# A chunked delta-rule scan: the recurrence's values transposed for four chunks at a time

## The chip, the cores and the metric

The kernel runs on one core of one Trainium2 chip, as one program. The metric is the device time of one execution in microseconds (us), the median over several. TensorE (PE in the profile) multiplies matrices into PSUM; VectorE (DVE), ScalarE (ACT) and GpSimd (POOL) do the elementwise work and the copies; transfers are issued from the queues of SyncE (SP), ACT and POOL.

## The reference

One encoder block on 512 frames of 1024 values, batch 1, float32. What matters here is the middle of it, where two token mixers run on one projection:

```
x = x + 1/2 * SwiGLU(RMSNorm(x))                    (first FFN)
p = RMSNorm(x) @ W_in
y_A = RWKV7(token-shifted columns of p) @ P_A       (8 heads x 64)
y_B = ForgettingAttention(other columns) @ P_B      (8 heads x 64)
x = x + (sigmoid(g_A)*y_A + sigmoid(g_B)*y_B) @ W_out
x = x + 1/2 * SwiGLU(RMSNorm(x))                    (second FFN)
out = RMSNorm(x)

RWKV7, per head, frame by frame, with a 64x64 state S:
S_t = S_{t-1} diag(w_t) + (S_{t-1} a_t) b_t^T + v_t k_t^T
y_t = S_t r_t
```

## The kernel before

**The stages.** In the order of time: the first FFN, the projection W_in with the preparation of the mixers' operands, the **scan** (the recurrence in chunks, with the attention and the last columns of the projection woven into it), the output projections, the second FFN. Float32 products are computed as three products of float32r parts: each weight tile is cast (`whi`, ACT, line 133) and its rest is formed (`wlo`, DVE, line 134), and `mm3` (line 142) multiplies high by high, high by low and low by high.

**The scan.** The 512 frames are cut into 16 chunks of 32 frames (`C` = 32, `NC` = 16), and heads into four pairs (`NP` = 4). For all heads at once the inverse of a triangular 32x32 matrix per chunk is formed ahead of it on DVE (lines 1249 to 1254, tile `TT`), written to memory and read back in another layout (line 1255 to `Td`, line 1261 into `Tall`). Then the loop over the chunks c does on PE: `read` (`xps`, line 1565: what the state and the values say at this chunk), `ups` (line 1611: times the inverse), `sps` (line 1638: the next state) and `yps` (line 1644: the output). The operand of `sps`, `yps` and `xps` is a tile `R` of 128 partitions per head, which holds the state, the solved rows and the values of the chunk. There are four such tiles, `Rs[0]` to `Rs[3]` (the names `RD` in the profile), used in turn, and four `Ds` for keys and decay.

**The values.** They lie transposed, features by frames, in the tiles `vs` (`V` in the profile). `stage_v(c)` transposes on PE the values of chunks c and c+1 for the four pairs of heads (four transposes of 64 frames into the PSUM tile `vp`, line 1366) and ACT copies them from there into two tiles `R` (four copies of 32 partitions by 256 elements, line 1370). `stage_b(c)` does the like for keys (`bp`, lines 1375 and 1379). `staged(c)` calls the one for even c and the other for odd c, two chunks ahead: `stage_v` runs at c = 0, 2, 4, ... 12 for the chunks 2, 4, 6, ... 14, and once before the loop for chunk 0. For c = 1, 2, 6 and 10 the call stands before `read(c)`, for c = 4 behind the first products of the iteration, otherwise ahead of them.

**What is woven in.** `some(n)` issues n steps of three matmuls of the remaining projections: 13 tasks of 8 steps, four `pq` and nine `pgt`, whose weights are cast and split one task ahead. The attention of one pair of heads runs in three units; a unit's logits (`lp`, line 1438) and softmax weights (`pts`, an exponential on ACT in line 1449, here called *the exponentials*) belong to one iteration, its transposes (`turned`, line 1463), copies (`tr`, line 1468) and values (line 1477) to the next. Small work that belongs to none of these (casts and splits of weights, evacuations, normalisation) waits in a list `side` and is issued by `flush`.

**What sets the order.** The matmuls of the scan are kept in program order; the instructions of the other engines are ordered by a scheduler from their dependences and its own estimates, at build time. Each engine then works through its own list in that fixed order. `tc.issue_after(i)` puts the instructions of its block that run on i's engine behind i. PSUM tiles of the scan come from a pool of three banks (`pr`): a new tile waits until the tile three allocations earlier has been read.

Of the kernel before, what the change touches and what calls it, by code (L numbers as in the profile page):

```python
# [9 lines left out]
F32 = mybir.dt.float32  # L10
F32R = mybir.dt.float32r
BF16 = mybir.dt.bfloat16
AF = mybir.ActivationFunctionType
# [5 lines left out]
P = 128  # L19
# [6 lines left out]
NP = DA // P  # L26
C = 32
NC = T // C
NB = T // P
# [22 lines left out]
def kernel(  # L52
# [7 lines left out]
    dve, act, pool, pe = nc.vector, nc.scalar, nc.gpsimd, nc.tensor  # L60
# [6 lines left out]
    pr = ctx.enter_context(tc.tile_pool(name="pr", bufs=3, space=PSUM))  # L67
# [11 lines left out]
    ident = cp.tile([P, P], F32, name="ident")  # L79
# [183 lines left out]
    with tc.tile_pool(name="x0", bufs=1) as x0:  # L263
        keep = tc.keep_in_program_order
# [436 lines left out]
    keep = tc.keep_in_program_order  # L701
# [310 lines left out]
    with ExitStack() as mx:  # L1012
        rp = mx.enter_context(tc.tile_pool(name="rp", bufs=1))
        sctx = ExitStack()
        sp = sctx.enter_context(tc.tile_pool(name="sp", bufs=1))
# [91 lines left out]
        vs = [V4[:, p] for p in range(NP)]  # L1107
# [141 lines left out]
        for t in range(C - 1):  # L1249
            n, m = t + 1, C - 1 - t  # L1250
# [7 lines left out]
        for i in range(2):  # L1258
            for q in range(2):
                o = i * 64 + q * C  # L1260
# [59 lines left out]
        for b in range(NB):  # L1320
            o = vts[b]
# [38 lines left out]

        keep = tc.keep_in_program_order

        def stage_v(c, keep=keep):
            vp = pr.tile([P, NP, 2, 64], F32, tag="b", name="vp")
            for p in range(NP):
                keep(pe.transpose(vp[0:64, p].rearrange("p a b -> p (a b)"), vs[p][:, c * C:(c + 2) * C], ident[:]))
            for j in range(2):
                for q in range(2):
                    o = 32 + (1 - q) * 64
                    act.copy(Rs[(c + j) % 4][o:o + 32, :, q, :], vp[j * C:(j + 1) * C, :, q, :])  # L1370

        def stage_b(c, keep=keep):
            bp = pr.tile([P, NP, 2, 64], F32, tag="b", name="bp")
# [48 lines left out]
        class Unit:  # L1422
# [19 lines left out]
            def weights(s):  # L1442
                for q in range(2):
                    pt, mx = pts[:, q], pairs[s.p][2][q]
                    for b in s.bl:
                        n, mb = (b + 1) * P, mx[:, b:b + 1]
                        l = s.lps[q][:, s.at[b]:s.at[b] + n]
                        dve.tensor_reduce(mb, l, axis=AX.X, op=ALU.max, negate=True)
                        act.activation(pt[:, s.at[b]:s.at[b] + n], l, AF.Exp, bias=mb, accum_out=mx[:, NB + b:NB + b + 1])

            def scaled(s):
                for q in range(2):
# [103 lines left out]
        for part in (stage_v, stage_b):  # L1556
            part(0, lambda i: i)
        some_of = [(2, 1, 3), (3, 3, 2)] + [(2, 1, 3), (3, 1, 2), (4, 2, 2), (2, 1, 3), (2, 1, 3), (2, 1, 3)] + [(4, 2, 2), (2, 1, 3), (2, 1, 3), (2, 1, 3), (4, 3, 3), (2, 1, 3), (2, 1, 3), (2, 1, 3)]

        def read(c):  # L1560
            R = Rs[c % 4]
            xps = pr.tile([P, 2, 64], F32, tag="b", name="xps")
            for p, q in heads():
                o = (p // 2) * 64 + q * C
                keep(pe.matmul(xps[o:o + C, p % 2, :], G[p][q][:, c, 0, :], R[:, p, q, :], start=True, stop=True,
                               tile_position=(0, o)))
            Xs = sp.tile([P, 2, 64], F32, tag="Xs", name="Xs", bufs=2)
            return Xs, dve.tensor_copy(Xs[:], xps[:])
# [12 lines left out]
        def unit(n):  # L1581
            return units[places.index(n)] if n in places else None

        def staged(c):
            if c + 2 < NC:
                (stage_b if c % 2 else stage_v)(c + 2 - c % 2)

        parted.extend((0, n, part) for n, part in enumerate(first_parts))
        with tc.issue_after(ahead.ins):
            Xs, taken = read(0)  # L1590
        for c in range(NC):
            R, Rn, Dt = Rs[c % 4], Rs[(c + 1) % 4], Ds[c % 4]
            cs = slice(c * C, (c + 1) * C)
            u, v = unit(c - 1), unit(c)
            n = some_of[c]
            late_logits = v and c == 12
            if c not in (1, 2, 4, 6, 10):
                staged(c)
            with tc.issue_after(taken.ins):
                flush(100 if c in (1, 12) else 5)  # L1600
            some(n[0])
            if c == 4:
                staged(c)
            if u:
                u.turned()
            elif c == 0:
# [49 lines left out]
            if c + 1 < NC:  # L1656
                Xs, taken = read(c + 1)
# [257 lines left out]
```

## Time and profile before

| | |
|---|---|
| time, median of 3 runs | 1135.68 us (1135.48 to 1136.68) |
| profiled execution, its own time | 1136.47 us |
| its span, first to last instruction | 1134.8 us |
| granted TensorE clock, mean | 0.998 |
| the scan's loop within the span | about 532 to 684 us |
| PE busy / DVE / ACT in 531 to 684 us (153 us) | 152.65 / 103.43 / 116.38 us |

How it is read: the span lies inside the time of the execution, 1.7 us shorter. PE's busy time is the time in which at least one matmul is in flight by a model of its ends; PEld is the loading of weights into the array, which precedes each matmul, and the idle times of PEld with what ended them show where PE's sequence stood. A row of the timeline gives start, duration, engine, line, operation, output and inputs, the count of merged instructions, and in brackets the idle time before it with its releaser.

### The profile page before, as it was taken

The page shows a single profiled execution, that of the slowest core. Times are in us where ns is not written, and L with a number is a line of the kernel's source. Part 1 is how long each engine was busy: PE and PEld are TensorE (multiplying, and loading weights), DVE is VectorE, ACT ScalarE, POOL GpSimd, SP SyncE. Part 2 cuts the span into 40 slices and gives each one's busy share as a digit, 9 for nine tenths or more (in the row PEclk, how much of TensorE's full clock was granted, in tenths as well). Part 3 has the DMA queues.
Part 4 walks back from the last instruction along what each step waited for, and adds up shares of the span by engine and source line. Part 5 has one row for each costly group of instructions (what it writes and reads, how often), then busy time and mean ns, then how long its engine had stood idle before and what let it go on. Part 6 is the DMA issues. An engine that isn't in the chain of part 4 may idle for free.

```text
span 1134.8 us, 19652 instructions
## 1 busy us (share of the span) xinstructions
PE 1125.1 (99%) x7782; PEld 990.5 (87%) x7782; DVE 865.3 (76%) x1372; ACT 614.1 (54%) x1029; POOL 98.6 (9%) x168
## 2 busy tenths in 40 slices
PE   9999999999999999999999999999999999999997
PEld 7899999988887888888777777888999999988887
DVE  6889999977666888767776668879999999943243
ACT  6646655643345754355877757536555566532121
POOL 2000000010000111321000011132000000010000
PEclk9999999999999999999999999999999999999999
DMA  8433333353333333345113136544333333363322
GB/s 261 135 93 96 111 112 96 111 176 121 118 111 112 101 105 101 113 140 144 33 44 104 64 113 202 176 148 127 97 100 105 111 96 112 107 193 92 90 78 75
DMA packets 211018, 131.17 MB, mean 116 GB/s; under 512 B 10446, under 2 KB 201486, under 8 KB 210926
## 3 DMA queue, kind: packets, MB, share of 16 engines
q1 hardware_dynamic: 202366, 108.67, 32.9%
q0 software_dynamic: 6320, 20.45, 5.4%
q8 instruction: 61, 1.00, 0.4%
q10 hardware_dynamic: 2240, 0.79, 0.3%
q14 instruction: 31, 0.25, 0.1%
HBM read 115.02 MB, written 14.88 MB: 114 GB/s over the span
## 4 chain that ended last, share of the span: by engine, by line
PE 96%; DVE 1%; ACT 1%; DMA 1%; issue 0%; SPq 0%; DVEq 0%; ACTq 0%
PE za L142 23%; PE pd L142 17%; PE zc L142 14%; PE pgt L142 8%; PE pk L142 6%; PE ppj L1691 4%; PE pw L142 4%; PE pq L142 3%; PE pb L142 3%; PE pa L142 3%; PE pv L142 2%; PE pl L142 1%; DMA xin<-in_x_dram 1%; PE lp L1477 1%; PE gp L1206 1%; PE lp L1463 1%
## 5 line engine op out<-in xcount | busy, mean ns | idle before, releaser
L133 ACT CAST whi<-raw 128x1024 fp32r<-128x1024 f32 (+2 forms) x114 | 110.6, 971 | 178.9 <-PE pd L142 88.1
L134 DVE TENSOR_TENSOR wlo<-raw,whi 128x1024 fp32r<-128x1024 f32 (+2 forms) x114 | 128.3, 1125 | 73.2 <-ACT whi L133 72.8
L142 PE MATMUL pd<-hh,wlo 128*128 128x512 f32 (+1 forms) x272 | 100.5, 370 | 0.0
L142 PE MATMUL pd<-hh,whi 128*128 128x512 f32 (+1 forms) x272 | 100.1, 368 | 0.0
L142 PE MATMUL pd<-hl,whi 128*128 128x512 f32 (+1 forms) x272 | 100.0, 368 | 0.0
L142 PE MATMUL zc<-xh,whi 128*128 128x256 f32 x296 | 83.8, 283 | 0.0
L142 PE MATMUL zc<-xl,whi 128*128 128x256 f32 x296 | 83.8, 283 | 0.0
L142 PE MATMUL zc<-xh,wlo 128*128 128x256 f32 x296 | 83.8, 283 | 0.0
L142 PEld LDWEIGHTS pd<-hl,whi 128*128 128x128 f32 x272 | 51.3, 189 | 8.4
L142 PEld LDWEIGHTS pd<-hh,wlo 128*128 128x128 f32 x272 | 51.3, 189 | 8.1
L142 PEld LDWEIGHTS pd<-hh,whi 128*128 128x128 f32 x272 | 51.3, 189 | 8.0
L504 ACT CAST wtwo<-wsum 128x1024 fp32r<-128x1024 f32 x37 | 38.9, 1050 | 33.3 <-PE za L142 33.3
L142 PEld LDWEIGHTS zc<-xh,whi 128*128 128x128 f32 x296 | 56.8, 192 | 0.0
L142 PEld LDWEIGHTS zc<-xl,whi 128*128 128x128 f32 x296 | 56.8, 192 | 0.0
L142 PEld LDWEIGHTS zc<-xh,wlo 128*128 128x128 f32 x296 | 56.8, 192 | 0.0
L142 PE MATMUL pgt<-xh,whi 128*128 128x512 f32 x128 | 53.0, 414 | 0.0
L507 DVE TENSOR_TENSOR wlo<-raw,whi 128x1024 fp32r<-128x1024 f32 x41 | 50.0, 1219 | 2.5 <-ACT whi L504 2.5
L516 DVE TENSOR_TENSOR wsum<-wsum,raw 128x512 f32<-128x512 f32 x74 | 50.9, 688 | 1.2
L516 DVE TENSOR_TENSOR wsum<-raw 128x512 f32<-128x512 f32 x74 | 50.6, 684 | 0.0
L142 PE MATMUL pgt<-xh,wlo 128*128 128x512 f32 x128 | 50.2, 392 | 0.0
L142 PE MATMUL pgt<-xl,whi 128*128 128x512 f32 x128 | 50.0, 391 | 0.0
L504 ACT CAST whi<-raw 128x1024 fp32r<-128x1024 f32 x41 | 43.1, 1052 | 9.0 <-PE zc L142 8.1
(582 smaller groups left out, 3490.8 us busy)
## 6 DMA issues: line engine op xcount, KB each, us to landing
raw<-in_ffn_w_dram SPq DMA_DIRECT2D x118, 512.0 KB
raw<-in_w_in_dram SPq DMA_DIRECT2D x40, 512.0 KB
raw<-in_ffn_w_dram SPq DMA_DIRECT2D x15, 384.0 KB
xP<-xpark POOLq DMA_DIRECT2D x16, 256.0 KB, 4.9
raw<-in_w_out_dram SPq DMA_DIRECT2D x8, 512.0 KB
gsave<-gs SPq DMA_DIRECT2D x9, 256.0 KB
xin<-in_x_dram SPq DMA_DIRECT2D x4, 512.0 KB
xpark<-xT POOLq DMA_DIRECT2D x8, 256.0 KB, 5.9
```

The costliest lines, as they stand in the source:

```text
L133: marks["wide"] = act.copy(hi[:], raw[:])
L134: marks["rest"] = (eng or dve).tensor_tensor(lo[:], raw[:], hi[:].bitcast(F32), op=ALU.subtract)
L142: mm = pe.matmul(ps, w, x_, start=first and n == 0, stop=last and n == 2, skip_group_check=chain)
L504: keep(act.copy(dst, src))
L507: keep(dve.tensor_tensor(dst, src, f32(hi), op=ALU.subtract))
L516: keep(dve.tensor_tensor(to, a, b, op=ALU.add))
L1206: gm = pe.matmul(gps[g][o, c], BK[s, cc], G[p][q][s, cc], start=True, stop=True)
L1463: keep(pe.transpose(s.lps[q][:, k * P:(k + 1) * P], pts[:, q, k * P:(k + 1) * P], ident[:]))
L1477: keep(pe.matmul(av[half(q), j * P:(j + 1) * P], vt[k][:, h * 64:(h + 1) * 64], s.trs[q][:, o:o + P], start=k == 0, stop=k == b))
L1691: keep(pe.matmul(ps[:], a[:, k, :], y[k][b], start=k == 0 and n == 0, stop=k == NP - 1 and n == 2))
```

## The change

`stage_v` transposes the values of four chunks at a time, for c divisible by four: the PSUM tile `vp` is now written on all 128 partitions. ACT copies the first two chunks from it as before, and DVE copies the other half (64 partitions by 512 elements) into a new SBUF tile `vkept`, from which ACT fills the `R` tiles of the other two chunks when `stage_v` is called for them. The call for c = 4, which now has no transposes, moves to the head of the iteration. Beside that, in iterations with an attention unit the block of `flush` stands behind the last exponential of the unit before, so that ACT work which `flush` issues comes later in ACT's order than that exponential.

```diff
+        vkept = []
         def stage_v(c, keep=keep):
-            vp = pr.tile([P, NP, 2, 64], F32, tag="b", name="vp")
-            for p in range(NP):
-                keep(pe.transpose(vp[0:64, p]..., vs[p][:, c * C:(c + 2) * C], ident[:]))
+            if c % 4 == 0:
+                vp = pr.tile([P, NP, 2, 64], F32, tag="b", name="vp")
+                for p in range(NP):
+                    keep(pe.transpose(vp[:, p]..., vs[p][:, c * C:(c + 4) * C], ident[:]))
+                src = vp
+            else:
+                src = vkept.pop()
             for j in range(2):
+                i = (c + j) % 4
                 for q in range(2):
                     o = 32 + (1 - q) * 64
-                    act.copy(Rs[(c + j) % 4][o:o + 32, :, q, :], vp[j * C:(j + 1) * C, :, q, :])
+                    act.copy(Rs[i][o:o + 32, :, q, :], src[i * C:(i + 1) * C, :, q, :])
+            if c % 4 == 0:
+                kept = sp.tile([P, NP, 2, 64], F32, name="vkept", tag="vkept")
+                dve.tensor_copy(kept[64:128], vp[64:128])
+                vkept.append(kept)
...
-                        act.activation(pt[...], l, AF.Exp, bias=mb, accum_out=...)
+                        s.exp = act.activation(pt[...], l, AF.Exp, bias=mb, accum_out=...)
...
-            if c not in (1, 2, 4, 6, 10):
+            if c not in (1, 2, 6, 10):
                 staged(c)
-            with tc.issue_after(taken.ins):
+            with tc.issue_after(taken.ins), tc.issue_after(u.exp.ins) if u else ExitStack():
                 flush(100 if c in (1, 12) else 5)
             some(n[0])
-            if c == 4:
-                staged(c)
```

The change was announced as joined to the first FFN's second product in pairs of output tiles; the diff holds nothing of that, and outside the preparation of the scan and the scan itself the instructions stand in the same order in both kernels.

What it does to the order of instructions, at three places. On PE the only difference in the whole program are the transposes `vp`: 32 before, 16 now, all other matmuls in the same order. At the head of iteration c = 0 (`xps` is the last of `read(0)`, `pq` the first woven product), before:

```order
L1565 MATMUL xps<-RD_5396,G_3854 32x64
L1565 MATMUL xps<-RD_5396,G_3855 32x64
L1366 MATMUL vp<-ident,V_4016 64x128 x4
L142 MATMUL pq<-xh_3768,whi 128x512
L142 MATMUL pq<-xl_3769,whi 128x512
```

and now:

```order
L1576 MATMUL xps<-RD_5396,G_3854 32x64
L1576 MATMUL xps<-RD_5396,G_3855 32x64
L142 MATMUL pq<-xh_3768,whi 128x512
L142 MATMUL pq<-xl_3769,whi 128x512
L142 MATMUL pq<-xh_3768,wlo 128x512
```

The four transposes are gone there; the same holds at c = 4, 8 and 12.

On DVE, at the end of the inversion ahead of the scan (`TT` is its result, `wlo` the rest of a weight of the projection), before:

```order
L1252 TENSOR_TENSOR prod<-TT,Ls 128x31
L1254 TENSOR_TENSOR TT<-TT,prod 128x31
L1283 TENSOR_TENSOR qk_5202<-qk_5202,rstd 128x512
L1283 TENSOR_TENSOR qk_5235<-qk_5235,rstd 128x512
L1336 SCALAR_TENSOR_TENSOR nf<-la,nf 8x512
L134 TENSOR_TENSOR wlo<-raw,whi 128x1024
```

and now:

```order
L1252 TENSOR_TENSOR prod<-TT,Ls 128x31
L134 TENSOR_TENSOR wlo<-raw,whi 128x1024
L1254 TENSOR_TENSOR TT<-TT,prod 128x31
L1283 TENSOR_TENSOR qk_5202<-qk_5202,rstd 128x512
L1283 TENSOR_TENSOR qk_5235<-qk_5235,rstd 128x512
L1336 SCALAR_TENSOR_TENSOR nf<-la,nf 8x512
```

The rest `wlo` of one weight has moved ahead of the last step of the inversion (the first copy into `vkept` stands earlier in the same chain).

On ACT, from iteration c = 7 into c = 8 (`tr` copies attention weights, lines 1615 and 1616 copy the solved rows into `R`, lines 1401 and 1402 cast attention operands, 1449 are the exponentials), before:

```order
L133 CAST whi<-raw 128x1024
L1468 COPY tr<-lp 128x384 x2
L1615 COPY RD_5397<-ups 32x2x64
...
L1402 CAST qb_5420<-qk_5619 64x512
L1449 ACTIVATE pts,mx_5945<-lp,mx_5945 128x512
L1449 ACTIVATE pts,mx_5946<-lp,mx_5946 128x512
L1295 ACTIVATE qrn<-pq_6364,epsr 128x512
L1296 ACTIVATE qrn<-qrn 128x512
L1648 COPY V_4016<-yps 128x4x32
L1501 ACT_TABLE_LOAD
L1501 ACTIVATE gs<-gs 128x512
L1370 COPY RD_5397<-vp 32x4x64 x4
```

and now:

```order
L1479 COPY tr<-lp 128x384 x2
L1624 COPY RD_5397<-ups 32x2x64
...
L1460 ACTIVATE pts,mx_5944<-lp,mx_5944 128x512
L1460 ACTIVATE pts,mx_5945<-lp,mx_5945 128x512
L133 CAST whi<-raw 128x1024
L1412 CAST qa_6412<-qk_5616 64x512
...
L1295 ACTIVATE qrn<-pq_6360,epsr 128x512
L1377 COPY RD_5397<-vkept 32x4x64
L1657 COPY V_4016<-yps 128x4x32
L1377 COPY RD_5397<-vkept 32x4x64
L1296 ACTIVATE qrn<-qrn 128x512
L1512 ACT_TABLE_LOAD
```

The cast `whi` and the four operand casts now stand behind the exponentials, and two of the four copies into `R` have moved up (the other two stand in the iteration before).

More of the change, by code (lines that the diff above doesn't have):

```diff
@@ L1361 @@
         keep = tc.keep_in_program_order
+        vkept = []
         def stage_v(c, keep=keep):
-            vp = pr.tile([P, NP, 2, 64], F32, tag="b", name="vp")
-            for p in range(NP):
-                keep(pe.transpose(vp[0:64, p].rearrange("p a b -> p (a b)"), vs[p][:, c * C:(c + 2) * C], ident[:]))
+            if c % 4 == 0:
+                vp = pr.tile([P, NP, 2, 64], F32, tag="b", name="vp")
+                for p in range(NP):
+                    keep(pe.transpose(vp[:, p].rearrange("p a b -> p (a b)"), vs[p][:, c * C:(c + 4) * C], ident[:]))
+                src = vp
+            else:
+                src = vkept.pop()
             for j in range(2):
+                i = (c + j) % 4
                 for q in range(2):
                     o = 32 + (1 - q) * 64
-                    act.copy(Rs[(c + j) % 4][o:o + 32, :, q, :], vp[j * C:(j + 1) * C, :, q, :])
+                    act.copy(Rs[i][o:o + 32, :, q, :], src[i * C:(i + 1) * C, :, q, :])
[3 more added lines that the diff above has]
+                vkept.append(kept)
         def stage_b(c, keep=keep):
@@ L1448, in weights @@
                         dve.tensor_reduce(mb, l, axis=AX.X, op=ALU.max, negate=True)
[L1449 removed]
+                        s.exp = act.activation(pt[:, s.at[b]:s.at[b] + n], l, AF.Exp, bias=mb, accum_out=mx[:, NB + b:NB + b + 1])
             def scaled(s):
```

## The prediction

> **What bounds the kernel now.** I read the page first, then the idle times of weight loading in the scan, then the timeline around each transpose that goes.
>
> ```profile
> span 1134.8 us, 19652 instructions
> PE 1125.1 (99%) x7782; PEld 990.5 (87%) x7782; DVE 865.3 (76%) x1372; ACT 614.1 (54%) x1029; POOL 98.6 (9%) x168
> PE 96%; DVE 1%; ACT 1%; DMA 1%; issue 0%; SPq 0%; DVEq 0%; ACTq 0%
> ```
>
> 96% of the chain that ended last is PE. So a matmul taken out of PE's sequence shortens the run by what it holds there, unless a wait fills the place; and freeing ACT or DVE brings only what PE waited for them. The waits of PE's weight loads in 480 to 690 us (us in total, times, longest):
>
> ```profile
> PEld sps L1638 <- issue: 3.1, 9, 0.4
> PEld ups L1611 <- issue: 2.6, 12, 0.4
> ...
> PEld sps L1638 <- ACT RD L1616: 0.7, 2, 0.4
> ...
> PEld pgt L142 <- DVE wlo L134: 0.3, 1, 0.3
> ...
> PEld lp L1438 <- ACT tr L1468: 0.2, 1, 0.2
> ```
>
> The first two belong to the changes between wide and narrow matmuls: nearly every `sps` has 0.35, whoever is named, and every `ups` 0.17 or 0.36. So the two 0.35 put down to ACT's line 1616 are that same gap and not a wait that could be won. Real waits are the last two rows and little else: at most some 0.7 us can be won beside the transposes.
>
> **The four groups of transposes that go** (c = 0, 4, 8, 12). Each group of four with the first matmul behind it:
>
> ```profile
> 533.11 0.62 PE L1366 MATMUL vp<-ident,V 128*64 128x128 f32 x4
> 533.50 0.48 PE L142 MATMUL pq<-xh,whi 128*128 128x512 f32 x1
> ...
> 573.91 0.60 PE L1366 MATMUL vp<-ident,V 128*64 128x128 f32 x4
> 574.34 1.04 PE L1463 MATMUL lp<-ident,pts 128*128 128x128 f32 x8
> ...
> 609.26 0.63 PE L1366 MATMUL vp<-ident,V 128*64 128x128 f32 x4
> 609.64 0.48 PE L142 MATMUL pgt<-xh,whi 128*128 128x512 f32 x1
> ...
> 645.90 0.63 PE L1366 MATMUL vp<-ident,V 128*64 128x128 f32 x4
> 646.28 0.48 PE L142 MATMUL pgt<-xh,whi 128*128 128x512 f32 x1
> ```
>
> From the start of a group to the start of what follows: 0.39, 0.43, 0.38 and 0.38, together **1.58 us**. The listed durations overlap; they are not the price.
>
> **The four groups that stay** load 128 columns of weights each where they loaded 64. The nearest row is `bp`, four such transposes before `xps`, against `vp` in the same place:
>
> ```profile
> 540.39 0.42 PEld L1375 LDWEIGHTS bp<-ident,BK 128*128 128x128 f32 x4
> 541.04 0.32 PEld L1565 LDWEIGHTS xps<-RD,G 128*32 128x32 f32 x16 [0.23 <-issue]
> 550.77 0.36 PEld L1366 LDWEIGHTS vp<-ident,V 128*64 128x64 f32 x4 [0.18 <-ACT qrn L1295]
> 551.48 0.32 PEld L1565 LDWEIGHTS xps<-RD,G 128*32 128x32 f32 x16 [0.34 <-PE vp L1366]
> ```
>
> The loads take 0.06 longer, but to the start of `xps` it is 0.65 with `bp` and 0.71 with `vp`: the gap may swallow it. Cost between 0 and 4 x 0.06 = 0.24; I take 0.1.
>
> **DVE's four copies into `vkept`.** The trace has no such copy of 512 elements. Copies out of PSUM show 0.28 us for 128 elements and 0.41 for 256, so 0.13 for each 128 more gives about 0.67. Three of them (c = 2, 6, 10) come just ahead of the unit's maxima, where DVE idled:
>
> ```profile
> 610.77 0.28 DVE L1482 COPY qk<-lp 128x128 f32<-128x128 f32 x1
> 600.78 0.41 DVE L1482 COPY qk<-lp 128x256 f32<-128x256 f32 x1
> 594.35 1.04 DVE L1448 TENSOR_REDUCE mx<-lp 128x1 f32<-128x384 f32 x2 [1.16 <-PE lp L1440]
> ```
>
> The 1.16 of c = 6 is the smallest of the three idle times, and it holds 0.67: no cost. Without that cover the maxima and the exponentials behind them would be 0.67 late, which PE needs only an iteration later; `sps`, which also needs the bank, comes some 3 us on. The first copy lies in the inversion, which is the next part.
>
> **The inversion ends later.** Now the weight rest that waits for the cast at 521.74 stands ahead of the last step of the inversion:
>
> ```profile
> 521.74 1.06 ACT L133 CAST whi<-raw 128x1024 fp32r<-128x1024 f32 x1 [3.91 <-PE pq L142]
> 522.16 0.36 ACTq L1255 DMA_DIRECT2D Td<-TT  x1
> 524.00 1.23 DVE L134 TENSOR_TENSOR wlo<-raw,whi 128x1024 fp32r<-128x1024 f32 x1
> L1261 POOL DMA_DIRECT2D Tall<-Td x2: 797/806/814, 525.8 to 526.6; - x2
> Tall<-Td POOLq DMA_DIRECT2D x2, 128.0 KB, 6.0
> 536.00 0.32 PEld L1611 LDWEIGHTS ups<-Xs,Tall 64*64 64x64 f32 x8 [0.37 <-issue]
> ```
>
> The cast ends at 522.80, 1.23 for the rest, 0.22 for the last step: the inverse is there at 524.3 instead of 522.1, 2.2 late. Its way through memory took from 522.16 to 526.6 + 6.0 = 532.6 and would now end at 534.8. The first `ups` comes at 536.0 - 0.39 = 535.6. Behind it stands everything on PE, but 0.8 us are left: no cost in the likeliest case. If transfers collide (the weight buffer is free 1.2 us earlier, so a load of 512 KB meets the write of `Td`) or the four staging copies of 0.36 hold up ACT's queue ahead of the issue, I bound it at 1.0.
>
> **ACT's new order.** Two real waits should go:
>
> ```profile
> 555.98 0.19 PEld L1438 LDWEIGHTS lp<-kb,qa 128*128 128x128 f32 x1 [0.23 <-ACT tr L1468]
> 602.98 0.19 PEld L142 LDWEIGHTS pgt<-xh,wlo 128*128 128x128 f32 x1 [0.26 <-DVE wlo L134]
> ```
>
> At c = 2 the cast `whi` (1.05) and a square leave the place ahead of `tr`: 0.23. At c = 7 a `slo` of 0.68 no longer stands ahead of the `wlo` that PE waits for: 0.26. Together between 0 and **0.49**; I take all of it.
>
> One wait is new. From c = 7 into c = 8 ACT has no reserve:
>
> ```profile
> 604.05 1.29 DVE L1448 TENSOR_REDUCE mx<-lp 128x1 f32<-128x512 f32 x2 [1.12 <-PE lp L1440]
> 606.79 0.69 ACT L1449 ACTIVATE pts<-lp,mx 128x512 f32<-128x512 f32 x1
> 616.12 0.26 ACT L1616 COPY RD<-ups 32x128 f32<-32x128 f32 x1
> 616.80 0.55 PEld L1638 LDWEIGHTS sps<-RD,RD 128*64 128x64 f32 x16 [0.35 <-ACT RD L1616]
> ```
>
> Before, the copies into `R` of c = 7 ended at 604.5 and those of c = 8 at 616.4 (616.12 + 0.26): 11.9 us of ACT without idle, and just in time for `sps` with its usual gap. Now the copies of c = 7 end at about 604.1 (the cast `whi` ahead of them is gone, but they wait for PE), and the exponentials, which come next, must wait for the first maximum: 604.05 + 0.65 and a signal, 604.8. From there the same list, with the `whi` put in (1.05) and two staging copies of 0.36 gone, takes 11.9 + 1.05 - 0.7 = 12.2 us and ends at 617.0, or 616.8 where the steps run a little closer: 0.5 late. PE without its transposes would be 0.38 early. So the gain of c = 8 is lost again: **0.5**, bounds 0 and 0.7. At c = 4 the same order has cover, the wait for transposes that are gone; at c = 12 ACT's order hardly changes:
>
> ```profile
> 574.54 1.49 ACT L1370 COPY RD<-vp 32x256 f32<-32x256 f32 x4 [1.23 <-PE vp L1366]
> 566.30 1.04 ACT L133 CAST whi<-raw 128x1024 fp32r<-128x1024 f32 x1
> 572.28 1.22 DVE L134 TENSOR_TENSOR wlo<-raw,whi 128x1024 fp32r<-128x1024 f32 x1
> ```
>
>
> Weight casts move behind exponentials at c = 2, 3, 6, 7 and 13. The tightest is that of c = 3: from 566.30 it goes behind two exponentials that cannot start before 567.3 and ends at about 569.7, and DVE comes to the rest at 572.28: 2.6 us of cover. If it went, the rest and PE's next product would be late by the excess.
>
> **The sum.** -1.58 + 0.1 - 0.49 + 0.5 = -1.5 us: span 1134.8 - 1.5 = 1133.3, and the profiled execution 1136.47 would be 1135.0. The median of the runs shown is 1135.68, 0.8 less than that execution; the same step gives **1134.2 us**, 0.13% less. Best bounds: -1.58 - 0.49 = -2.1; worst: -1.58 + 0.24 + 0.7 + 1.0 = +0.4. A measurement of this kernel cannot tell less than about 0.2%, 2.3 us, from no change, so the likeliest verdict is *no change*.
>
> **The rivals.**
>
> A, *the transposes hold PE for their listed duration*:
>
> ```profile
> L1366 PE MATMUL vp<-ident,V x32: 270/272/300, 488.1 to 646.3; 128*64 128x128 f32 x32
> ```
>
> 16 x 0.272 = 4.35 us, less the same corrections, gives 1131.4. For it speaks only that duration; against it the four starts within 0.4 us. The Trainium skill, in "TensorE: Matmul & The Clock Gate", section "Part 4: PE-mode transpose", gives about 275 ns for a 128x128 transpose within a kernel; taken as a price per transpose it leads to this rival, and the rows' spacing says that it is a latency. Chance 4%.
>
> B, *nothing is left*: the first `ups` waits the full 1.0 and ACT is late at c = 8 by 0.7, and no old wait goes: -1.58 + 0.1 + 0.7 + 1.0 = +0.2, 1135.9. For it: both reserves are under 1 us. Against: each needs its bound. Chance 17%.
>
> C, *the inverse arrives far too late, and the kernel is slower*. The window 515 to 540 us counts small packets, which this relayout in rows of 32 elements makes:
>
> ```profile
> DMA packets 7295, 3.80 MB, mean 152 GB/s; under 512 B 2224, under 2 KB 7037, under 8 KB 7293
> ```
>
> It now starts at another phase of the weight loads. If the read into `Tall` shares the engines with loads for its whole length and doubles, it lands 6.0 later; less the 0.8 of reserve, 5.2 us stand in front of the whole loop: -1.5 + 5.2 = +3.7, 1139.4. The kernel is slower from a way 2.3 longer on (0.8 + 1.5), the verdict from 4.6 on. Against it: a load already lay in that stretch before. Chance 10%.
>
> D, *more is won than the rows name*: with ACT's order freed, gaps called "issue" shrink too. If a quarter of the 5.7 us of them before `sps` and `ups` goes, 1.4 more: 1132.8. Against it: they stand where no engine is late. Chance 9%.
>
> **Chances and range.** The forecast has 60%, its own range 1133.2 to 1135.2 (the scatter of the three runs is 1.2 us wide). Of it a sixth lies beyond 2.3 us of gain. Faster by over 0.2%: 10 + 4 + 6 from D = 20%; slower: 8 from C, 2 from B and 1 from the scatter = 11%; within: 69%. The range of 8 in 10: from D, 1132.7, to B with half a scatter, 1136.5.
>
> **What would show it.** PE's transposes `vp` 16, each removed group's neighbours 0.4 us closer. The first `ups` without a wait for a transfer, its issue of `Td` at about 524.3. No wait of `lp` at c = 2 for `tr`, none of `pgt` at c = 7 for `wlo`. `sps` of c = 8 with a gap of about 0.85 instead of 0.35. DVE's new copies 0.67 each. The stages behind the scan as long as before, all 1.5 us earlier. It is wrong if PE waits for `Tall`, if another `sps` grows a gap, or if the scan's end moves by something else than 1.5 us.

## The result, and the profile after

The changed kernel takes **1134.03 us** in the median (1133.61 to 1135.57), the kernel before beside it 1135.80 us (1135.19 to 1137.41). The ratio is 0.9985, with a 95% interval of 0.9979 to 0.9991: 1.77 us or 0.15% less, which stays inside the 0.2% that the prediction named as the limit. Forecast were 1134.2 us and no change.

The profiled spans differ by more, 1134.8 against 1132.2 us. The head of the page after, and its chain of waits:

```profile
span 1132.2 us, 19627 instructions
PE 1123.5 (99%) x7766; PEld 990.0 (87%) x7766; DVE 867.4 (77%) x1376; ACT 615.3 (54%) x1029; POOL 98.5 (9%) x168
PE 98%; DVE 1%; ACT 0%; issue 0%; DVEq 0%
```

Sixteen matmul records fewer, and the 1% of DMA that stood in the chain before is gone. That 1% is the transfer of the input `xin` in the first 14 us, far ahead of what the change touches. Ahead of the scan PE's sequence is the same in all the kernels below, yet the first `xps` of the scan starts anywhere between 531.79 and 533.46 us in thirteen profiled executions (532.74 before, 531.91 after). Its earliest row, from the kernel with ACT's order alone, and its latest, from the kernel with the transposes alone:

```profile
531.79 0.28 PEld L1565 LDWEIGHTS xps<-RD,G 128*32 128x32 f32 x16 [0.35 <-issue]
```

```profile
533.46 0.28 PEld L1576 LDWEIGHTS xps<-RD,G 128*32 128x32 f32 x16 [0.35 <-issue]
```

All but 0.3 us of the difference arises in the first 30 us, at the transposes of the input and the first sums behind them, and it is as large as the whole gain. Two spans cannot be compared here. What can be compared is the time of each matmul *after that first `xps`*: with the kernel before as the measure, it repeats to some 0.03 us from one kernel's execution to another's wherever the edits change nothing. The table below is made so, from the start times on PE.

In the timeline of PE after, `xps` is now followed at once by the woven product (c = 0 and c = 8):

```profile
531.91 0.44 PE L1576 MATMUL xps<-RD,G 128*32 128x64 f32 x16
532.28 0.50 PE L142 MATMUL pq<-xh,whi 128*128 128x512 f32 x1
...
606.86 0.45 PE L1576 MATMUL xps<-RD,G 128*32 128x64 f32 x16
607.23 0.50 PE L142 MATMUL pgt<-xh,whi 128*128 128x512 f32 x1
```

The waits of PE's weight loads after, in 480 to 690 us:

```profile
...
PEld ups L1620 <- issue: 2.9, 14, 0.4
PEld sps L1647 <- issue: 2.7, 8, 0.4
PEld xps L1576 <- issue: 1.8, 9, 0.4
PEld xps L1576 <- PE vp L1369: 0.8, 3, 0.3
...
PEld sps L1647 <- ACT RD L1625: 0.4, 1, 0.4
```

`lp <- tr` and `pgt <- wlo` have left the list, as forecast. No wait for `Tall` has come into it, and the gaps called "issue" before `sps` and `ups` have hardly shrunk (5.6 for 5.7). At c = 8 the new delay is there, in another shape than forecast. The weight loads there:

```profile
614.38 0.73 PEld L1647 LDWEIGHTS sps<-RD,RD 128*64 128x64 f32 x15 [0.35 <-ACT RD L1625]
...
616.58 0.28 PEld L1576 LDWEIGHTS xps<-RD,G 128*32 128x32 f32 x16 [0.17 <-issue]
```

The gap is the usual 0.35, but the loads behind it take 0.73 and more instead of 0.55: two of ACT's four copies into `R` had ended (at 614.25), the other two had not. ACT's last copy into `R`:

```profile
614.55 0.26 ACT L1625 COPY RD<-ups 32x128 f32<-32x128 f32 x1
```

It ends at 614.81, 0.43 after PE had begun `sps`.

### The profile page after: what moved, and what is told of

Read it like the earlier page. It is cut to its first block, busy times and chain, and to the rows that moved or that the text cites. A ratio compares the mean times of both kernels' runs of the same rounds, so it can differ in the third digit from the quotient of the medians.

```text
span 1132.2 us, 19627 instructions
## 1 busy us (share of the span) xinstructions
PE 1123.5 (99%) x7766; PEld 990.0 (87%) x7766; DVE 867.4 (77%) x1376; ACT 615.3 (54%) x1029; POOL 98.5 (9%) x168
## 4 chain that ended last, share of the span: by engine, by line
PE 98%; DVE 1%; ACT 0%; issue 0%; DVEq 0%
PE za L142 23%; PE pd L142 17%; PE zc L142 14%; PE pgt L142 8%; PE pk L142 6%; PE ppj L1700 4%; PE pw L142 4%; PE pq L142 4%; PE pb L142 3%; PE pa L142 3%; PE pv L142 2%; PE pl L142 1%; PE f L309 1%; PE lp L1488 1%; PE gp L1206 1%; PE sps L1647 1%
## 5 line engine op out<-in xcount | busy, mean ns | idle before, releaser
L504 ACT CAST whi<-wsum 128x1024 fp32r<-128x1024 f32 x37 | 38.8, 1049 | 17.1 <-PE zc L142 13.2
```

The lines of the kernel that those rows point to most:

```text
L504: keep(act.copy(dst, src))
```

## The experiments

In the table: what each kernel gains (-) or loses (+) against the kernel before up to the place named, counted from the first `xps`, in us; below that the difference of the medians. "four" is the transposes alone, "order" ACT's order alone, "padded" and "padded behind" the changed kernel with unused transposes put back, "held", "c8", "pool" and "qrn" variants that are told below.

```
place            after   four  order  padded  p.behind  held    c8   pool   qrn
ups, c = 0       -0.34  -0.34   0.00    0.00    0.00   -0.34  -0.34  -0.34  -0.34
sps, c = 2       -0.32  -0.08  -0.32   -0.31   -0.33   -0.11  -0.31  -0.33  -0.09
ups, c = 4       -0.43  -0.43  +0.01   +0.90   +0.03   -0.43  -0.43  -0.43  -0.44
sps, c = 7       -0.13  +0.29  -0.02   -0.13   -0.13   -0.02  +0.30  -0.01  +0.29
xps, c = 8        0.00  +0.71   0.00    0.00    0.00    0.00  +0.70   0.00   0.00
ups, c = 8       -0.38  -0.37  +0.95   +0.95   +0.05   -0.38  -0.38  -0.38  -0.38
xps, c = 9       +0.24   0.00   0.00    0.00    0.00    0.00   0.00   0.00   0.00
sps, c = 12      -0.39  -0.39   0.00    0.00    0.00   -0.39  -0.38  -0.39  -0.39
all other places +0.04  +0.04  +0.11   +0.12    0.00   +0.02   0.00  +0.07  +0.03
the loop         -1.71  -0.57  +0.73   +1.53   -0.38   -1.65  -0.84  -1.81  -1.32
behind the loop  -0.03   0.00  +0.65   -0.02    0.00   -0.02  -0.03  -0.05  +0.22
medians          -1.77  -0.80  +1.28   +1.39   -0.31   -1.66  -1.40  -2.40  -1.21
```

The table explains the medians to some 0.3 us. In "c8" and "pool" the medians are 0.5 lower than the sums: the kernel before ran at 1136.3 beside them instead of 1135.8. Between these two, which ran together, the medians differ by 1.00 and the sums by 0.99.

**The two halves of the change, each alone.** First the transposes by four without the new order; the call for c = 4 stays at its old place (the edit against the changed kernel):

```diff
-            with tc.issue_after(taken.ins), tc.issue_after(u.exp.ins) if u else ExitStack():
+            with tc.issue_after(taken.ins):
                 flush(100 if c in (1, 12) else 5)
...
```

> The transposes by four alone, without the new place of the exponentials and with the call for c = 4 at its old place. The price-of-the-slot theory (each removed group of four transposes gives back the 0.38 to 0.43 us that it held between its neighbours): -1.4 to -1.6 us against the kernel before, the four steps of about -0.38 at c = 0, 4, 8, 12 in the places of the trace; the wait of 0.23 of lp for tr at c = 2 and that of 0.26 of pgt for wlo at c = 7 stay; no loads of sps stretched at c = 8, so that c = 8 keeps its 0.38. Rival O (the gain is ACT's new order): 0.0 against before. Rival A (transposes hold their listed 0.272 each): -4.3.

Measured 1135.03 us, ratio 0.9993 (0.9984 to 1.0002), 0.80 less than before instead of 1.4 to 1.6. The four steps came as expected (-0.34, -0.43, -0.37, -0.39). The two waits that were to stay did not. At c = 2 `lp` no longer waits for `tr`, but soon behind it `pq` waits for DVE, so that only 0.08 is won:

```profile
559.08 0.19 PEld L1291 LDWEIGHTS pq<-slo,bonesr 128*128 128x128 f32 x1 [0.41 <-DVE slo L158]
```

At c = 7 `pgt` no longer waits for `wlo`, although `flush` stands where it stood before the change: DVE now forms this `wlo` ahead of a `slo` that stood ahead of it before.

```profile
601.02 1.22 DVE L134 TENSOR_TENSOR wlo<-raw,whi 128x1024 fp32r<-128x1024 f32 x1
602.15 0.68 DVE L158 TENSOR_TENSOR slo<-qsq,shi 128x512 fp32r<-128x512 f32 x1
```

Not expected either was a loss of 1.0 us around c = 8. Two new waits of PE's weight loads make it:

```profile
604.03 0.19 PEld L1449 LDWEIGHTS lp<-kb,qa 128*128 128x128 f32 x1 [0.34 <-ACT tr L1479]
...
609.79 0.29 PEld L1576 LDWEIGHTS xps<-RD,G 128*32 128x32 f32 x16 [0.88 <-ACT qrn L1295]
```

And ACT's timeline of the same kernel ahead of them:

```profile
599.12 0.40 ACT L1377 COPY RD<-vkept 32x256 f32<-32x256 f32 x1
...
600.48 0.40 ACT L1377 COPY RD<-vkept 32x256 f32<-32x256 f32 x1
600.90 1.51 ACT L1390 COPY RD<-bp 64x256 f32<-64x256 f32 x4
602.43 1.05 ACT L133 CAST whi<-raw 128x1024 fp32r<-128x1024 f32 x1
603.50 0.86 ACT L1479 COPY tr<-lp 128x384 f32<-128x384 f32 x2
```

The copies of c = 8 no longer wait for a transpose, since `vkept` lies in SBUF. So two of them run in the iteration before, and `tr` ends 2.41 us behind the start of `ups` of c = 7 instead of 1.40.

Then the order alone (the edit against the kernel before; the line that names `s.exp` goes with it):

```diff
-            with tc.issue_after(taken.ins):
+            with tc.issue_after(taken.ins), tc.issue_after(u.exp.ins) if u else ExitStack():
                 flush(100 if c in (1, 12) else 5)
```

> The new order of ACT alone: the kernel before, with its 32 transposes, and flush behind the last exponential. Price-of-the-slot theory: the waits at c = 2 and c = 7 (0.23 and 0.26) go, at c = 8 ACT is late because two staging copies of 0.36 and the cast of 1.05 now both stand in its list: 0.3 to 1.0 lost at sps of c = 8; in sum between -0.4 and +0.6 against before. Rival O: about -1.7.

Measured 1137.11 us, ratio 1.0011 (1.0002 to 1.0020): 1.28 *slower*, where +0.6 was the most that was expected. The 0.32 at c = 2 is there. The wait at c = 7, which was to go, is still there, with `slo` ahead of `wlo` as before:

```profile
601.79 0.19 PEld L142 LDWEIGHTS pgt<-xh,wlo 128*128 128x128 f32 x1 [0.27 <-DVE wlo L134]
```

And at c = 8 the transposes wait as they never did before:

```profile
609.02 0.36 PEld L1366 LDWEIGHTS vp<-ident,V 128*64 128x64 f32 x4 [1.06 <-DVE Xs L1568]
```

Another 0.33 is lost behind the loop, where `yc` waits 0.56 for DVE instead of 0.23, and 0.37 at the program's last products; that last loss was not followed up. So one half gains 0.57 in the loop, the other loses 0.73, and both together gain 1.71. The rival that the gain is ACT's order has fallen with this run, but so has the simple sum of two independent halves.

**The transposes put back.** The changed kernel with four groups of four transposes into a tile that nobody reads, at the four places from which they went:

```diff
         def stage_v(c, keep=keep):
+            if c % 4:
+                ballast(c)
...
+        def ballast(c):
+            wp_ = pr.tile([P, NP, 2, 64], F32, tag="b", name="ballast")
+            for p in range(NP):
+                keep(pe.transpose(wp_[0:64, p].rearrange("p a b -> p (a b)"), vs[p][:, c * C:(c + 2) * C], ident[:]))
```

> The changed kernel, with four unused transposes of 64 frames put back on PE at each of the four places from which they went (c = 0, 4, 8, 12); the lists of ACT, DVE and POOL are those of the changed kernel. Price-of-the-slot theory: +1.3 to +1.6 against the changed kernel (four groups by 0.38, less 0.25 where the wait at c = 8 is covered again), so -0.2 to -0.5 against before. Rival O: as the changed kernel, -1.7 against before. Rival A: +4.3 against the changed kernel, +2.6 against before.

Measured 1137.22 us, ratio 1.0013 (1.0004 to 1.0022), so 3.2 above the changed kernel instead of 1.3 to 1.6. At c = 0 and c = 12 a group costs 0.34 and 0.39; at c = 4 and c = 8 it costs 1.33, and again the wait names `Xs`:

```profile
571.06 0.36 PEld L1388 LDWEIGHTS ballast<-ident,V 128*64 128x64 f32 x4 [1.06 <-DVE Xs L1586]
...
610.08 0.36 PEld L1388 LDWEIGHTS ballast<-ident,V 128*64 128x64 f32 x4 [1.06 <-DVE Xs L1586]
```

The transposes use nothing that DVE makes there. Nor have ACT, DVE or GpSimd another list than in the changed kernel: in the built programs they are equal, instruction by instruction. What the transposes share with `Xs` is PSUM: `Xs` is DVE's copy out of the tile `xps`. The built programs name the bank of each tile of the pool `pr` (the head sums `pq2` lie in it too). Around c = 8:

```
                   before  order  padded  four  after
pq2 (head sums)       3      3      3      3      2
sps, c = 7            4      2      4      2      3
yps, c = 7            2      4      2      4      4
xps, c = 8            3      2      4      3      3
vp or ballast         4      2      4      -      -
```

The banks are not used in turn, as I had taken it when I described the kernel before: they are given out at build time, and it looks as if a new tile gets the one that is free first by the scheduler's estimate. Before, `xps` takes the bank of `pq2` and leaves the transposes the free one of `sps`. In "order" and "padded" `xps` takes the bank of `sps`, and the transposes right behind are given the bank that `xps` has just filled. PE then stands until DVE has emptied it. At c = 4 of "order" the two share a bank as well and nothing is lost: there the transposes stand behind the first products. That the change of ACT's order is what shifted the banks follows from "order", which has no other edit; the rule of choice itself I only infer.

**The same padding behind the products.** If that is so, the groups of c = 4 and c = 8 must cost their plain price where the copy is long done (the groups of c = 0 and c = 12 stay at the head):

```diff
...
             some(n[0])
+            if c in (4, 8):
+                ballast(c + 2)
             if u:
                 u.turned()
```

> The changed kernel with the same four groups of unused transposes as in e3_after_padded, but those of c = 4 and c = 8 put behind the first woven products instead of at the head of the iteration. Bank theory (at the head the group's PSUM bank is the one that xps has just filled, and PE stands 1.06 us until DVE has copied it; behind the products that copy is long done): c = 4 and c = 8 cost 0.43 each instead of 0.90 + 0.43 and 0.95 + 0.38, so +1.5 to +1.7 against the changed kernel, some 1.6 to 1.9 less than e3_after_padded. Rival (the padding made ACT or DVE late): still about +3.2 against the changed kernel.

Measured 1135.47 us, ratio 0.9997 (0.9988 to 1.0006), 1.4 above the changed kernel, a little under the 1.5 to 1.7 expected, since the 0.24 lost at c = 8 is covered again. The groups of c = 4 and c = 8 cost 0.46 and 0.43, and the rows have no wait (the weight loads of c = 4):

```profile
572.89 0.56 PEld L1388 LDWEIGHTS ballast<-ident,V 128*64 128x64 f32 x4
573.45 0.91 PEld L1481 LDWEIGHTS lp<-ident,pts 128*128 128x128 f32 x8
```

Both tiles still have the bank of `xps` in this program; only the time has passed. The 1.06 are the price of the bank, the rival of a late ACT or DVE is out. And with its 16 transposes back the changed kernel is by the table 0.38 faster in the loop than the one before. Of that 0.33 is the wait at c = 2, which ACT's order wins alone too; the 0.13 at c = 7 it does not win alone, and this comes with the copies from `vkept`, as is told further down.

**The price of a group in numbers.** Two groups behind the products of each of the 16 iterations:

```diff
...
             some(n[0])
+            ballast(c // 2 * 2)
+            ballast(c // 2 * 2)
```

> The changed kernel, with two groups of four unused transposes behind the woven products of each of the 16 iterations, 32 groups or 128 transposes in all: the price of a group where PE stands at its limit. Price-of-the-slot theory: 32 x 0.38 = +12.2 us against the changed kernel, some less where a group covers a wait. Rival A: 128 x 0.272 = +34.8. Rival O (the transposes stand in the shadow of other work): under +3.

Measured 1148.32 us, ratio 1.0109 (1.0095 to 1.0123). In the loop this kernel is 13.87 above the changed one (+12.16 against -1.71; 12.2 was expected), 32 x 0.433, and each iteration shows its own step of 0.85 to 0.90. The listed durations in this kernel:

```profile
L1386 PE MATMUL ballast<-ident,V x128: 270/272/273, 534.1 to 689.4; 128*64 128x128 f32 x128
```

128 x 0.272 would be 34.8. So a transpose in such a group holds PE for 0.108, four tenths of what its row lists. Rival A is out. The Trainium skill's 275 ns for a 128x128 transpose in bf16 within a kernel ("TensorE: Matmul & The Clock Gate", section "Part 4: PE-mode transpose") agrees with the 272 listed here for fp32; it is the duration of one, and no sum can be made of it.

**What ACT's order is good for.** "four" lost 1.0 at c = 7 and 8. In "held" its copies from `vkept` are put behind the last exponential, and the casts stay where they were. (The edit reaches c = 8 and c = 12; the call for c = 4, which the expectation names too, stands elsewhere and was left as it was.)

```diff
             if c not in (1, 2, 4, 6, 10):
-                staged(c)
+                with tc.issue_after(u.exp.ins) if u and c % 4 == 0 else ExitStack():
+                    staged(c)
```

> e1_four_only with one thing more: for c = 4, 8 and 12 the copies from vkept into R stand behind the last exponential of the unit before. Theory of the early copies (in e1_four_only two of them, 0.40 us each, ran ahead of the cast whi at c = 7, in ACT's fullest stretch, and made tr, the square root's inverse and with it PE late by 0.29 and 0.71): both losses go, about -1.5 against before, 0.7 less than e1_four_only. Rival (the whole new order of ACT, with the casts behind the exponentials, is needed): as e1_four_only, -0.8 against before.

Measured 1134.12 us, ratio 0.9988 (0.9979 to 0.9997): as fast as the changed kernel, and -1.66 against before for the -1.5 expected. The whole order with the casts is not needed. With the early copies the gain at c = 7 goes too: `slo` stands ahead of `wlo` again, and `pgt` waits 0.26. So it is these copies that turn the two on DVE. In the kernels with them on ACT ahead of c = 7's `tr` (after, "four", the two padded ones, "c8", "qrn") `wlo` comes first and the wait is gone; in those without ("order", "held", "pool") it stays. Why the scheduler turns them stays open. But the built program shows a second difference, which the expectation had not seen: `xps` of c = 8 has bank 2 here, that of `sps`, where "four" has bank 3, that of `pq2`, which ACT's `qrn` reads. The 0.88 before `xps` in "four" names just this `qrn`. So the run does not say whether the copies or the bank cost the 0.71.

"qrn" tells them apart: "four" with its early copies, and `qrn` of c = 7 put *later*, behind ACT's copy of the output. That gives `xps` of c = 8 bank 2:

```diff
             if ends:
-                ends()
+                with tc.issue_after(out_copy.ins) if c == 7 else ExitStack():
+                    ends()
```

> e1_four_only with one thing more: at c = 7 the square root's inverse qrn stands on ACT behind the copy of the output V, so later than in e1_four_only; in the built program xps of c = 8 thereby gets the PSUM bank that sps of c = 7 left, and no longer that of the head sums pq2 which qrn reads. The two copies from vkept stay early. Bank theory (the 0.71 us before xps of c = 8 is a wait for that bank, and not a price of ACT's lateness): the 0.71 goes although qrn comes later, 0.29 at c = 7 (lp for tr) stays: -1.2 to -1.3 against before, 0.7 less than e1_four_only with equal starts. Theory of the early copies alone (xps waits for work on ACT that the copies made late): 0.7 or more stays, -0.8 or worse.

Measured 1134.54 us, ratio 0.9990 (0.9981 to 0.9999), -1.21 against before, as the bank theory has it; 0.22 is lost behind the loop, which was not followed up. ACT's row of `qrn` and PE's rows, in two views:

```profile
608.79 0.69 ACT L1295 ACTIVATE qrn<-pq,epsr 128x512 f32<-128x512 f32 x1
```

```profile
602.92 0.19 PEld L1449 LDWEIGHTS lp<-kb,qa 128*128 128x128 f32 x1 [0.34 <-ACT tr L1479]
...
607.97 0.28 PEld L1576 LDWEIGHTS xps<-RD,G 128*32 128x32 f32 x16 [0.17 <-issue]
```

`xps` starts 0.8 before `qrn` does and waits for nothing; the 0.29 for `tr` stays. So the early copies cost the 0.29, and without the bank of `pq2` there is no 0.71. (`qrn` belongs to the norms of the attention; `xps` has no use for its result.) But the bank alone does not cost it either: in the kernel before `xps` of c = 8 has that bank too, and it starts when `qrn` has just read it:

```profile
608.13 0.69 ACT L1295 ACTIVATE qrn<-pq,epsr 128x512 f32<-128x512 f32 x1
```

```profile
608.88 0.28 PEld L1565 LDWEIGHTS xps<-RD,G 128*32 128x32 f32 x16 [0.17 <-ACT qrn L1295]
```

`qrn` ends there at 608.82, 76.08 us behind the first `xps`. In "four" it ends at 609.74, 76.28 behind it: 0.20 later, with the early copies ahead of it on ACT. PE, which has fewer transposes to do, would have been there 0.52 sooner than before. These two make the 0.71. So the kernel before held this wait without any reserve, behind a gap that looks like the usual 0.17, and a faster PE could not gain there unless the bank changed or `qrn` came sooner.

**The delay left at c = 8.** "c8" leaves the new order out for c = 8 alone:

```diff
-            with tc.issue_after(taken.ins), tc.issue_after(u.exp.ins) if u else ExitStack():
+            with tc.issue_after(taken.ins), tc.issue_after(u.exp.ins) if u and c != 8 else ExitStack():
```

> The changed kernel with the new place of flush behind the last exponential left out for c = 8 alone. Theory (the 0.24 us lost at sps of c = 8 comes from the cast whi and the square root that now stand between the exponentials and the copies of the solved rows): that loss goes, -0.2 to -0.3 against the changed kernel, the rest unchanged to 0.05 at every other place; -0.13 at c = 7 may go too, since ACT's order there is the old one again. Rival (the early copies from vkept come back as in e1_four_only): +0.5 to +1.0 against the changed kernel.

Measured 1134.90 us, ratio 0.9988 (0.9979 to 0.9997). My theory fell and the rival came true (+0.87 against the changed kernel in the loop): the cast goes back ahead of `tr`, the early copies stand ahead of it (+0.30), `xps` has the bank of `pq2` (+0.70); the 0.24 is won and 1.0 lost. The 0.24 had to be won otherwise. "pool" gives the copies from `vkept` to GpSimd:

```diff
-                    act.copy(Rs[i][o:o + 32, :, q, :], src[i * C:(i + 1) * C, :, q, :])
+                    (act.copy if c % 4 == 0 else pool.tensor_copy)(Rs[i][o:o + 32, :, q, :], src[i * C:(i + 1) * C, :, q, :])
```

> The changed kernel with the 16 copies from vkept into R on GpSimd instead of ACT (they read SBUF now). ACT has 16 x 0.40 = 6.5 us less to do, 0.8 of it ahead of sps of c = 8: the 0.24 there goes, nothing else waits for ACT, -0.2 to -0.3 against the changed kernel. Rival (GpSimd's copies slow DVE's work on SBUF, or come too late for R): PE waits for DVE at other places, 0 to +1 against the changed kernel.

Measured 1133.90 us, ratio 0.9979 (0.9970 to 0.9988), the best of all. The loss of 0.24 is gone, but the gain of 0.13 at c = 7 is gone with it, since the early copies no longer stand on ACT; in the loop it is 0.10 ahead of the changed kernel instead of 0.2 to 0.3, which no timing of this kernel can show (the intervals overlap). The rival's waits for DVE did not come. GpSimd's copies of that kernel:

```profile
L1377 POOL COPY RD<-vkept x16: 392/396/865, 524.0 to 644.6; 32x256 f32<-32x256 f32 x16
```

**The reserve of the inverse.** The forecast put the end of its way 0.8 us ahead of the first `ups`. Two kernels delay it on GpSimd, by a copy of a part of the inverse or of all of it onto itself ahead of the write to `Td`:

```diff
+        pool.tensor_copy(TT[:, 0:8], TT[:, 0:8])
         tw = nc.scalar.dma_start(Td[:], TT)
```

(the other has `TT[:]`.)

> The changed kernel with a copy of 128 by 256 elements of the inverse onto itself on GpSimd ahead of its write to memory: the inverse about 1 us later, to measure the reserve of the first ups. If the reserve is the forecast 0.8 us of the kernel as it was predicted, or less: the first ups waits for Tall, +0.2 or more. If it is 1.8 us, as the landing of 4.2 us in the changed kernel's trace says: 0.0 at the first ups.

> The same with a copy of all 128 by 1024 elements: the inverse about 4 us later. With a reserve of 1.8 us: PE waits at the first ups for what the write is late beyond it, about +2 us (the trace of this run tells by how much the write is late, the wait should be that less 1.8); with a reserve of 0.8, one more. Rival (transfers have no part in it, or the read is hidden anyway): 0.0.

The small delay: 1134.07 us, ratio 0.9985 (0.9976 to 0.9994), as the changed kernel. Against the first `xps` the issue of `Td` is 0.79 later (523.44 before 531.91, now 524.59 before 532.27), and the first `ups` comes where it came. The rows of the issue, after and with the delay:

```profile
523.44 0.35 ACTq L1255 DMA_DIRECT2D Td<-TT  x1
```

```profile
524.59 0.36 ACTq L1256 DMA_DIRECT2D Td<-TT  x1
```

So the reserve is over 0.79. By the rows of the changed kernel it should be 1.8: the last read issued on GpSimd at 528.8 lands 4.2 us later, at 533.0, and the first `ups` starts at 534.83.

The large one: 1140.31 us, ratio 1.0039 (1.0025 to 1.0053), 6.3 above the changed kernel instead of about 2. `Td` is issued 3.15 later, and the reads on GpSimd go a further step back, behind a cast that the scheduler moved ahead of them. PE's weight loads, two of its products, and the table by stretches (stretch, length, busy time and instructions of the five engines; the third number from the end is PE's granted clock):

```profile
539.11 0.50 PEld L1621 LDWEIGHTS ups<-Xs,Tall 64*64 64x64 f32 x4 [3.83 <-DVE qk L1301]
539.91 0.49 PEld L1621 LDWEIGHTS ups<-Xs,Tall 64*64 64x64 f32 x4 [0.30 <-DMA Tall<-Td]
```

```profile
541.54 0.63 PE L142 MATMUL pq<-xh,wlo 128*128 128x512 f32 x1
...
544.52 0.39 PE L142 MATMUL pq<-xh,whi 128*128 128x512 f32 x1
```

```profile
520.00:535.00 15.00, 15.00 (x81) 12.12 (x80) 13.55 (x23) 8.41 (x14) 5.45 (x8) 1.00 0.48 127
535.00:539.00 4.00, 0.72 (x4) 0.23 (x2) 1.41 (x2) 2.30 (x4) 0.73 (x2) 0.84 1.15 205
539.00:541.00 2.00, 1.75 (x9) 1.47 (x10) 0.00 (x0) 0.35 (x2) 0.00 (x0) 0.50 1.04 317
541.00:543.00 2.00, 2.00 (x6) 1.52 (x6) 0.00 (x0) 1.94 (x6) 0.00 (x0) 0.50 0.08 19
543.00:545.30 2.30, 2.30 (x8) 1.52 (x6) 0.00 (x0) 0.91 (x2) 0.00 (x0) 0.67 0.00 0
545.30:548.00 2.70, 2.68 (x55) 2.23 (x55) 1.86 (x5) 1.18 (x4) 0.00 (x0) 1.00 0.00 0
```

The 3.83 are put down to DVE's `qk`, which was done at 538.5; the read that GpSimd issued at 533.57 landed 5.5 later, at 539.07, and that is when `ups` began; its second half waited another 0.30 for the second read. PE's products before had ended at 535.72, so PE stood for 3.42 us between products (3.83 between weight loads). The clock fell to half while it stood, at about 537.7 (1.3 us at half make the mean of 0.84 in the 4 us from 535), and stayed there until about 544.5, where the products take 0.39 again instead of 0.63. The stretch from `ups` to `sps` takes 6.20 us instead of the 3.34 of the changed kernel. So the wait cost 3.5, and the slow clock behind it, with the 0.30, another 2.84.

The Trainium skill has this rule ("TensorE: Matmul & The Clock Gate", section "Why this matters for your kernels": no idle gaps of PE above some 3 us, else the clock falls to half), and the trace agrees: 3.42 us without a product brought 0.50. Where the limit lies no run here shows.

## Why the prediction was right

The sum was right. Its largest term was right for the reason given, two smaller ones were off, and one of the waits went for another reason than the one forecast. Measured in the table, place by place:

| step of the prediction | forecast, us | measured, us |
|---|---|---|
| the four groups that go | -0.39, -0.43, -0.38, -0.38 | -0.34, -0.43, -0.38, -0.39 |
| the wide groups that stay | +0.1 (0 to 0.24) | 0.00 |
| waits at c = 2 and c = 7 | -0.23, -0.26 | -0.32, -0.13 |
| the new delay at c = 8 | +0.5 (0 to 0.7) | +0.24 |
| the inverse | 0 (to 1.0) | 0.00 |
| DVE's copies into `vkept` | 0.67 each, hidden | 0.69 each, hidden |
| all other places | none | +0.04 |
| the sum | -1.5 | -1.71 |

*The groups that go.* The distance between neighbours was the right price and the listed duration the wrong one; 128 transposes put in confirm it with 0.433 a group.

*DVE's copies* and ACT's from `vkept`, in the rows of that tile after:

```profile
L1377 ACT COPY RD<-vkept x16: 402/404/406, 522.5 to 644.2; 32x256 f32<-32x256 f32 x16
L1380 DVE COPY vkept<-vp x4: 694/694/695, 496.5 to 628.6; 64x512 f32<-64x512 f32 x4
```

*The groups that stay.* The gap swallowed the longer loads, and `xps` comes 0.71 behind the first load as before. The weight loads of the changed kernel at c = 2:

```profile
549.61 0.42 PEld L1369 LDWEIGHTS vp<-ident,V 128*128 128x128 f32 x4 [0.17 <-ACT qrn L1295]
550.32 0.32 PEld L1576 LDWEIGHTS xps<-RD,G 128*32 128x32 f32 x16 [0.29 <-PE vp L1369]
```

*The new delay at c = 8* had the right cause and was mis-sized: 0.24 for 0.5. Counted from PE's sequence the exponentials started when forecast, though they waited 0.19 for the maximum and not 0.7: an early copy from `vkept` of 0.40, which the forecast had not placed there, kept ACT busy until then. The list from there to the last copy took 12.03 us (602.78 to 614.81) and not 12.2, and half of `sps` could begin before that copy.

*The waits that go* were right in the sum, 0.45 for 0.49, in part by luck. At c = 2 the order alone shows the same 0.32. At c = 7 the forecast had `wlo` come ahead of `slo` through ACT's new order. The order alone leaves the two as they were and the wait in place; it is the early copies from `vkept` that turn them, and 0.13 is won and not 0.26.

*The inverse.* Its end moved as forecast (2.1 for 2.2). Its way was not 10.4 us as before but 9.6: the last read was issued 5.4 behind the write instead of 4.4, but it took 4.2 and not 6.0. The reserve was 1.8 by these rows, not 0.8. The zero was right with more room than stated, and rival B, which needed the full 1.0 there, had less ground than its 17%.

*Rival C* is a true mechanism that was not met here. It would have cost more than its price says: the forecast made the loss equal to the lateness beyond the reserve, and the run with the large delay shows 2.84 us on top of it, most of it from the slow clock. *Rival D* is out: the gaps called "issue" before `sps` and `ups` went from 5.7 to 5.6.

**What the prediction did not see** is that its two parts are not independent. It took the new order of ACT as a gain of its own of 0.49 less 0.5. The runs show that the transposes by four *without* it lose 1.0 at c = 7 and 8 (copies that no longer wait for PE run too early, and `xps` waits for a bank that before was free just in time), and that the order *without* the transposes by four loses 0.95 at c = 8 (a bank). That the sum came out in spite of this is luck: the banks of the changed kernel happen to fit, and with the transposes of c = 8 gone nothing is left there that could wait as in "order". The prediction never asked which bank a tile gets, though the description of the kernel names the pool of three.

## What to carry to other kernels

Price an instruction on a full engine by the distance between its neighbours, not by its listed duration. When a copy's source moves from PSUM to a buffer that is filled long before, ask where the copy will now run, since the wait that held it in place is gone. And where a scheduler picks buffers by its estimates, a wait that names an instruction whose result the waiting one does not use can be a buffer and not a dependence: look whose tile lay there, and move the reader or the tile and not the work. It can also be a name for something else that ended last, as `qk` was for a transfer above.

## What the runs showed of the hardware

- While PE stood for 3.42 us between products, its granted clock fell to 0.50, about 2 us behind the last product's end, and stayed there for some 7 us; products of 128x512 took 0.63 us in that time instead of 0.39.
- A copy of 32 by 256 elements from SBUF to SBUF takes ACT 0.404 us and GpSimd 0.396 in the median (one of its sixteen took 0.865), and ACT 0.36 to 0.37 where the source is PSUM (1.49 for the four that the prediction quotes). In the median GpSimd is no slower than ACT here.
- The read into `Tall` on GpSimd's queue, of the same bytes each time, took 6.0 us before and in the median 4.2 to 4.6 in the kernels with the transposes by four, where it starts some 3 us later counted from the first `xps`; with the largest delay it took 5.5. What makes the difference no run shows.
- The time to the first `xps` of the scan varies by 1.7 us over thirteen executions in which PE does the same work up to there, while behind it the executions agree to some 0.03 us wherever their kernels do the same.
